# Folding the Fourier mixer's tokens n and S-n ahead of the sequence transform

## The chip, the core and the metric

The kernel runs on one NeuronCore of a Trainium2 chip. The metric is the device time of one execution in microseconds (us). The engines are named as in the profile: PE (TensorE, matmuls; PEld is its weight load), DVE (VectorE), ACT (ScalarE), POOL (GpSimd) and SP (SyncE, whose queue issues most transfers). Each engine works its own queue of instructions, and they wait for each other by semaphores.

## What is computed

One encoder layer on two requests with the same weights: 512 prompt tokens (one tile, t = 0) and 1024 sample tokens (two tiles, t = 1 and 2), 1024 channels. The part that matters here is the Fourier mixer. Its input `f` is a 512-channel slice of the input projection of the normed activations, in 4 groups of 128 channels:

```
def fourier_mix(f):
    fg = f.reshape(b, s, N_FOURIER_GROUPS, FOURIER_GROUP_DIM).astype(jnp.float32)
    y = jnp.fft.fft2(fg, axes=(1, 3), norm="ortho").real
    return y.reshape(b, s, FOURIER_WIDTH).astype(f.dtype)
...
u = rms_norm(x, norm1_g)
proj = u @ w_in
f, q, k, v, g_ret, g_a, g_b = jnp.split(proj, ...)
branch_a = fourier_mix(f) @ w_four_proj
branch_b = bidirectional_retention(q, k, v, g_ret, ret_decay_logit) @ w_ret_proj
merged = jax.nn.sigmoid(g_a) * branch_a + jax.nn.sigmoid(g_b) * branch_b
```

The real part of the two-dimensional transform is cos·cos minus sin·sin: a channel transform by a table of 65 cosine and 63 sine columns, and a sequence transform by cosine and sine tables over the tokens.

## The kernel before

Every float32 product is made of float32r halves: `split(h, l, src)` rounds on ACT (L74) and takes the remainder on DVE (L75), and `mm3` issues three matmuls (L110 to L112). Weights and tables come as slabs: `slab(src)` issues a transfer on SP's queue (L93) and splits what it brings.

The program's start goes stage by stage. `Prep` fetches the input tiles of a request (`fetch`), makes the scaled halves `uh`, `ul` (`scale`, L195 and L196), the squares and their sums (`square`, L151/L153 and L157), the norm of each token as a column (`cols`: 4 matmuls with `ones`, L130, then `nr` by a power on POOL, L134) and as a row over all partitions (`rows`: 4 matmuls, L140). `f_proj(t, g)` projects a tile to one channel group (24 matmuls of 512 columns) and `f_evac` copies the bank to `ft` on ACT (L224). `channel_dft(si, pr)` multiplies, for sequence `si` and a pair of groups `pr`, each chunk of 128 tokens of `ft` by the channel table `cs` (plain float32, L249), and evacuates with the token's norm as a scale into `zh` (ACT, L255) and `zl` (DVE, L256). `sequence_dft(si, zts)` runs over the chunks of a sequence: 4 for the prompt, 8 for the sample, 258 columns per matmul, one table slab for two chunks (prompt) or one (sample); the channel 64 has a matmul group of its own with the 4-column tile `z64`. After that come the products with `wfour`, which also combine tokens n and S-n of the result.

Between these stand the constants of the retention stage: `de` (a power on POOL), a polynomial on DVE that ends in `dz`, the small tables `ex`, and three groups of powers on POOL: `qk_dec`, `g128` and, in `decay_d`, the decay matrices `D`, four of 128x256, each as four powers of 128x64:

```
for q in range(4):
    m = slice(64 * q, 64 * (q + 1))
    nc.gpsimd.tensor_tensor(D[:, m], two.broadcast_to([P, 64]), D[:, m], op=ALU.pow)
```

The instructions are written in the order of the stages, but a scheduler sets the order on each engine's queue, by what it takes each instruction to need; the pool `fp` with 13 buffers under the tag `f2` holds `xs`, `sq`, `ft`, `zh` and `zl` in turn, and a tile waits until its buffer is free.

Of the kernel before, what the change touches and what calls it, by code (L numbers as in the profile page):

```python
# [7 lines left out]
F32 = mybir.dt.float32  # L8
F32R = mybir.dt.float32r
AF = mybir.ActivationFunctionType  # L10
ALU = mybir.AluOpType
# [3 lines left out]
P = 128  # L15
KD = 8
TC = 512
# [5 lines left out]
SEQS = ((0, 4, 0, 1), (4, 8, 1, 2))  # L23
# [7 lines left out]
C_ID, C_CS, C_POS, C_SEL, C_END = 0, 128, 256, 260, 388  # L31
# [4 lines left out]
def emit(ctx, tc, x, wsl, wup, wdq, wd0, wfour, tab, cst, rcst, vec, out):  # L36
    nc = tc.nc
# [35 lines left out]
    def split(h, l, src):  # L73
        nc.scalar.copy(h, src)  # L74
        nc.vector.tensor_tensor(l, src, h.bitcast(F32), op=ALU.subtract)  # L75
# [33 lines left out]
    def mm3(o, lh, ll, rh, rl, first, last, go_on=False):  # L109
        nc.tensor.matmul(o, lh, rh, start=first, stop=False, skip_group_check=go_on)  # L110
        nc.tensor.matmul(o, ll, rh, start=False, stop=False, skip_group_check=go_on)  # L111
        nc.tensor.matmul(o, lh, rl, start=False, stop=last, skip_group_check=go_on)  # L112
# [31 lines left out]
    class SumSq:  # L144
        def __init__(self, first=None, pool=False):
            self.acc, self.first, self.pool = None, first, pool

        def add(self, src, pool=False):
            sq = (self.first if self.acc is None and self.first is not None else tmp("sq"))[:, :src.shape[1]]
            if self.pool or pool:  # L150
                nc.gpsimd.tensor_tensor(sq, src, src, op=ALU.mult)  # L151
            else:
                nc.scalar.activation(sq, src, AF.Square)  # L153
            if self.acc is None:
                self.acc = sq
            else:
                (nc.gpsimd if self.pool else nc.vector).tensor_tensor(self.acc, self.acc, sq, op=ALU.add)  # L157
# [16 lines left out]
    class Prep:  # L174
# [23 lines left out]
            u[self.t][1].append(l)  # L198

        def square(self, k):  # L200
            self.ss.add(self.xs[k], self.t == 1 and k % 2 == 1)
            self.xs[k] = None

        def cols(self):
# [14 lines left out]

    ft = {}  # L220

    def f_evac(t, g, ps):
        ft[t, g] = fp.tile([P, TC], F32, name="ft", tag="f2")
        nc.scalar.copy(ft[t, g], ps)  # L224

    def f_proj(t, g):
        ps = bank()
        for k in range(KD):
            f_mm(ps, g, t, k)
        f_evac(t, g, ps)  # L230


    pq = {}
    z64 = [[fp.tile([P, n, 4], F32R, name=f"z64{i}{n}", bufs=1) for i in range(2)] for _, n, _, _ in SEQS]

    def channel_dft(si, pr):
        c0, ncs, t0, nt = SEQS[si]
        zt = []
        for c2 in range(ncs // 2):
            ps = bank()  # L240
            zh = fp.tile([P, 512], F32R, name="zh", tag="f2")
            zl = fp.tile([P, 512], F32R, name="zl", tag="f2")
            for j in range(2):
                c = 2 * c2 + j
                b = slice(j * 256, (j + 1) * 256)
                o = ps[:, b].rearrange("p (q g j) -> p q g j", q=2, g=2)
                for gi in range(2):
                    src = ft[t0 + c // 4, 2 * pr + gi]
                    nc.tensor.matmul(o[:, :, gi], src[:, (c % 4) * P:(c % 4 + 1) * P],  # L249
                                     cs[:, C_CS:C_CS + P], start=True, stop=True)  # L250
            for j in range(2):
                c = 2 * c2 + j
                b = slice(j * 256, (j + 1) * 256)
# [7 lines left out]
            zt.append((zh, zl))  # L261
        return zt


    def sequence_dft(si, zts):
        c0, ncs, t0, nt = SEQS[si]
# [1 line left out]
        acc = {pr: [[bank(258) for _ in range(spans)] for _ in range(2)] for pr in zts}  # L268
        acc64 = [bank(258) for _ in range(spans)] if 1 in zts else []
        per = 4 // (2 * spans)  # L270
        for c in range(ncs):
            if c % per == 0:
                th, tl = slab(tab[si * 2 + c // per], 1032)
            b = (c % 2) * 256
            for pr, zt in zts.items():
                zh, zl = zt[c // 2]
                for q in range(2):
                    for s in range(spans):
                        col = ((c % per) * 2 * spans + q * spans + s) * 258
                        m = slice(b + q * P, b + (q + 1) * P)  # L280
                        args = (th[:, col:col + 258], tl[:, col:col + 258], c == 0, c == ncs - 1)
# [58 lines left out]
    for k in range(KD):  # L340
        preps[1].fetch()
    nc.sync.dma_start(cs, cst)
    for k in range(KD):
# [5 lines left out]
    preps[0].cols()  # L349
    for g in range(4):  # L350
        f_evac(0, g, fps[g])
    for k in range(KD):
        preps[1].scale()
        preps[1].square(k)


    def small(name, cols=16):
# [32 lines left out]
    f_proj(2, 1)  # L390
    preps[2].cols()
    l2 = const.tile([P, 16], F32, name="nv", tag="nv", bufs=1)
    nc.vector.tensor_scalar(l2, z, LOG2E, None, op0=ALU.mult)

# [45 lines left out]
        decay_d(hp)  # L440
    todo = [(t, g) for g in (2, 3) for t in (1, 2)]
    for i, _ in enumerate(sequence_dft(1, {0: z10})):
        if i % 2 == 0 and todo:
            f_proj(*todo.pop(0))
    state["turn"] = -1
    for q in preps:
        q.rows()
    z11 = channel_dft(1, 1)
    fill = gb_main(range(1), fp, "f2", 13)
    next(fill)  # L450
# [878 lines left out]
```

## Time and profile before

| | us |
|---|---|
| median of 3 runs (lowest, highest) | 2277.09 (2275.61, 2282.09) |
| the profiled execution | 2278.14 |
| its span in the trace | 2276.0 |
| PE busy | 2227.3 |
| DVE busy | 1475.6 |
| ACT busy | 848.3 |
| POOL busy | 345.5 |

The granted TensorE clock is 0.991 in the mean. In the profile, times in a timeline are counted from the start of the span; a row of it gives the start, the time from the first instruction's start to the last one's end, the engine, the line, the operation with its output and inputs, and in brackets how long the engine stood before it and for whom. A plain float32 matmul of 128 columns shows as two rows. The times of matmuls overlap, so the cost of one in a stream is read from start to start.

### The profile page before, as it was taken

To read this page: it belongs to the slowest core of one execution; us is meant where nothing else is said; L and a number is where in the kernel's file an instruction comes from. 1 tells how busy PE (TensorE), PEld (TensorE's weight loads), DVE (VectorE), ACT (ScalarE), POOL (GpSimd) and SP (SyncE) were. 2 spreads that over 40 slices of the span, in tenths; PEclk is the share of its full clock that TensorE was granted. 3 is DMA by queue.
4 is the path that set the end of the run, shared out by engine and by line. 5 is a ranking of instruction groups with operands and counts; after the bars stand their busy time and mean duration, and the time that the engine had idled before them with its cause. 6 is when DMAs were issued, how large, how long until landed. Compare 5 with 4: busy or idle time off the path is not lost. (4 is left out here: it accounts for less than half of the span.)

```text
span 2276.0 us, 29369 instructions
## 1 busy us (share of the span) xinstructions
PE 2227.3 (98%) x11294; PEld 1868.5 (82%) x11294; DVE 1475.6 (65%) x2555; ACT 848.3 (37%) x1373; POOL 345.5 (15%) x184
## 2 busy tenths in 40 slices
PE   8899999999999999999999999999998999999997
PEld 6788888888888888878887788888876778999986
DVE  7454434656556462245678886767699888999744
ACT  6251222223121221233334544434453445666423
POOL 2799601111212120010110000000000000000001
PEclk9999999999999999999999999999999999999999
DMA  5252220111102012276656462323264455323562
GB/s 190 66 164 90 92 86 2 47 38 38 47 14 71 1 56 79 74 241 226 226 181 226 147 215 90 114 93 116 84 235 144 153 203 195 106 99 112 170 205 70
DMA packets 103531, 273.30 MB, mean 120 GB/s; under 512 B 11488, under 2 KB 14816, under 8 KB 97760
## 3 DMA queue, kind: packets, MB, share of 16 engines
q1 hardware_dynamic: 99936, 265.15, 34.8%
q10 hardware_dynamic: 3456, 6.29, 0.7%
q8 instruction: 88, 1.44, 0.3%
q14 instruction: 51, 0.42, 0.1%
HBM read 208.22 MB, written 63.18 MB: 119 GB/s over the span
## 5 line engine op out<-in xcount | busy, mean ns | idle before, releaser
L111 PE MATMUL bank<-op,wl 128*128 128x512 f32 (+1 forms) x1320 | 463.8, 351 | 5.8 <-DVE wl L75 5.8
L110 PE MATMUL bank<-op,wh 128*128 128x512 f32 (+1 forms) x1320 | 462.4, 352 | 3.6 <-DVE y L1099 1.7
L112 PE MATMUL bank<-op,wh 128*128 128x512 f32 (+1 forms) x1320 | 462.1, 351 | 0.5 <-DVE op L75 0.5
L75 DVE TENSOR_TENSOR wl<-wr,wh 128x1024 fp32r<-128x1024 f32 (+5 forms) x210 | 250.9, 1196 | 161.6 <-ACT wh L74 159.4
L74 ACT CAST wh<-wr 128x1024 fp32r<-128x1024 f32 (+5 forms) x210 | 204.8, 976 | 321.3 <-PE bank L112 211.1
L110 PEld LDWEIGHTS bank<-op,wh 128*128 128x128 f32 x1320 | 250.3, 190 | 42.7 <-DVE y L1099 2.6
L111 PEld LDWEIGHTS bank<-op,wl 128*128 128x128 f32 x1320 | 250.5, 190 | 41.5 <-DVE wl L75 6.6
L112 PEld LDWEIGHTS bank<-op,wh 128*128 128x128 f32 x1320 | 250.7, 190 | 36.5 <-DVE op L75 1.2
L110 PE MATMUL bank<-uh,wh 128*128 128x512 f32 x672 | 271.8, 404 | 5.1 <-ACT wh L74 5.1
L111 PE MATMUL bank<-uh,wl 128*128 128x512 f32 x672 | 266.1, 396 | 0.7 <-DVE wl L75 0.6
L112 PE MATMUL bank<-ul,wh 128*128 128x512 f32 x672 | 266.3, 396 | 0.0
L134 POOL TENSOR_TENSOR nr<-nv,mhalf 128x4 f32<-128x4 f32 (+1 forms) x10 | 12.8, 1284 | 1105.4 <-DVE nv L133 1074.8
L74 ACT CAST wh<-wt 128x1024 fp32r<-128x1024 f32 (+2 forms) x120 | 117.3, 977 | 141.9 <-PE bank L112 130.1
L425 POOL TENSOR_TENSOR D<-two,D 128x64 f32<-128x64 f32 x16 | 170.1, 10659 | 0.0
L110 PE MATMUL bank<-wh,uh 128*128 128x512 f32 x384 | 166.8, 434 | 0.0
L110 PEld LDWEIGHTS bank<-uh,wh 128*128 128x128 f32 x672 | 126.9, 189 | 31.8 <-ACT wh L74 5.1
L111 PE MATMUL bank<-wh,ul 128*128 128x512 f32 x384 | 151.6, 395 | 0.0
L112 PE MATMUL bank<-wl,uh 128*128 128x512 f32 x384 | 151.2, 394 | 0.0
L112 PEld LDWEIGHTS bank<-ul,wh 128*128 128x128 f32 x672 | 126.7, 188 | 29.2
L111 PEld LDWEIGHTS bank<-uh,wl 128*128 128x128 f32 x672 | 126.9, 189 | 28.5 <-DVE wl L75 1.6
L75 DVE TENSOR_TENSOR wl<-wt,wh 128x1024 fp32r<-128x1024 f32 (+2 forms) x120 | 135.7, 1131 | 6.5 <-ACT wh L74 6.3
L310 DVE TENSOR_TENSOR sg<-bank,rrow 128x512 f32<-128x512 f32 x48 | 33.2, 691 | 164.4 <-PE bank L112 164.4
(233 smaller groups left out, 4113.3 us busy)
## 6 DMA issues: line engine op xcount, KB each, us to landing
wr<-wsl SPq DMA_DIRECT2D x92, 512.0 KB, 3.9
wr<-wup SPq DMA_DIRECT2D x44, 1024.0 KB, 4.9
xs<-x SPq DMA_DIRECT2D x48, 256.0 KB, 4.4
wr<-tab SPq DMA_DIRECT2D x18, 516.0 KB, 3.7
wr<-wdq SPq DMA_DIRECT2D x12, 768.0 KB, 4.2
wr<-wd SPq DMA_DIRECT2D x16, 512.0 KB, 4.3
sb<-sg ACTq DMA_DIRECT2D x24, 256.0 KB, 2.0
ma<-sg SPq DMA_DIRECT2D x24, 256.0 KB, 2.0
```

The costliest lines, as they stand in the source:

```text
L74: nc.scalar.copy(h, src)
L75: nc.vector.tensor_tensor(l, src, h.bitcast(F32), op=ALU.subtract)
L110: nc.tensor.matmul(o, lh, rh, start=first, stop=False, skip_group_check=go_on)
L111: nc.tensor.matmul(o, ll, rh, start=False, stop=False, skip_group_check=go_on)
L112: nc.tensor.matmul(o, lh, rl, start=False, stop=last, skip_group_check=go_on)
L134: nc.gpsimd.tensor_tensor(r, v, mhalf[:, 0:n], op=ALU.pow)
L310: nc.vector.tensor_tensor(sg, ps, rrow[t], op=ALU.mult)
L425: nc.gpsimd.tensor_tensor(D[:, m], two.broadcast_to([P, 64]), D[:, m], op=ALU.pow)
```

## The change

The input of the transform is real, so tokens n and S-n can be added (for the cosine part) or subtracted (for the sine part) before the sequence transform, which then needs half the tokens. The change does this inside the channel transform: `f_evac` multiplies the bank by the norm's row on DVE, writes the upper half of the sequence in reverse order into `ft`, puts the token S/2 into a column of its own, `fx`, and clears the column that has no partner by a memset on POOL. `channel_dft` issues two matmuls for each group, one with `cs` and one with `cr` (the cosine columns, and the sine columns negated) on the reversed half, into the same bank. The token S/2 comes in through a rank-one product with `mid`, a row of alternating 1 and -1. `sequence_dft` runs over half the chunks and half the table slabs, and asks for the next slab behind the matmuls of a chunk instead of ahead of the next one. Since `ft` now holds normed values, the norm's rows are needed early: `rows()` of each request is called before its first `f_evac`; the scaling in the channel transform's evacuation goes away. The squares of the tiles 1 and 2 are written in place.

```
-        def add(self, src, pool=False):
-            sq = (self.first if self.acc is None and self.first is not None else tmp("sq"))[:, :src.shape[1]]
+        def add(self, src, pool=False, inplace=False):
+            if inplace:
+                sq = src
+            else:
+                sq = (self.first if self.acc is None and self.first is not None else tmp("sq"))[:, :src.shape[1]]
...
     def f_evac(t, g, ps):
-        ft[t, g] = fp.tile([P, TC], F32, name="ft", tag="f2")
-        nc.scalar.copy(ft[t, g], ps)
-
-    def f_proj(t, g):
+
+        f = ft[t, g] = fp.tile([P, TC], F32, name="ft", tag="f2")
+        r = rrow[t]
+        lo = (TC // 2, TC, 0)[t]
+        if lo:
+            nc.vector.tensor_tensor(f[:, :lo], ps[:, :lo], r[:, :lo], op=ALU.mult)
+        if lo < TC:
+            nc.vector.tensor_tensor(f[:, lo + 1:], ps[:, TC - 1:lo:-1], r[:, TC - 1:lo:-1], op=ALU.mult)
+            nc.vector.scalar_tensor_tensor(fx[min(t, 1)][g], ps[:, lo:lo + 1], (TC * (1 + min(t, 1)) * 128.0) ** -0.5,
+                                           r[:, lo:lo + 1], op0=ALU.mult, op1=ALU.mult)
+            nc.gpsimd.memset(f[:, lo:lo + 1], 0.0)
...
     def channel_dft(si, pr):
         c0, ncs, t0, nt = SEQS[si]
+        half = ncs // 2
         zt = []
-        for c2 in range(ncs // 2):
+
+        for c2 in range(half // 2):
...
-                    src = ft[t0 + c // 4, 2 * pr + gi]
-                    nc.tensor.matmul(o[:, :, gi], src[:, (c % 4) * P:(c % 4 + 1) * P],
-                                     cs[:, C_CS:C_CS + P], start=True, stop=True)
-            for j in range(2):
-                c = 2 * c2 + j
-                b = slice(j * 256, (j + 1) * 256)
-                r = rcol[t0 + c // 4][:, c % 4:c % 4 + 1]
-                nc.scalar.activation(zh[:, b], ps[:, b], AF.Identity, scale=r)
-                nc.vector.scalar_tensor_tensor(zl[:, b], ps[:, b], r, zh.bitcast(F32)[:, b],
-                                               op0=ALU.mult, op1=ALU.subtract)
+                    g = 2 * pr + gi
+                    up = ft[t0 + nt - 1, g][:, (nt == 1) * 256:]
+                    m = slice(c * P, (c + 1) * P)
+                    nc.tensor.matmul(o[:, :, gi], ft[t0, g][:, m], cs[:, C_CS:C_CS + P], start=True, stop=False)
+                    nc.tensor.matmul(o[:, :, gi], up[:, m], cr, start=False, stop=True)
+            split(zh, zl, ps)
...
+        for gi in range(2):
+            nc.tensor.matmul(o[:, :, gi], fx[si][2 * pr + gi], cs[:, C_CS:C_CS + P], start=True, stop=True)
...
     def sequence_dft(si, zts):
...
-        for c in range(ncs):
-            if c % per == 0:
-                th, tl = slab(tab[si * 2 + c // per], 1032)
+        half = ncs // 2
+        mid = fp.tile([P, TC], F32R, name="mid", tag="f2")[0:1, :258]
+        nc.scalar.copy(mid.rearrange("p (a b) -> p a b", b=2), pm[0:1].unsqueeze(1).broadcast_to([1, 129, 2]))
+        table = slab(tab[si * 2], 1032)
+        for c in range(half):
+            th, tl = table
...
+            for pr, zt in zts.items() if c == 0 else ():
+                zh, zl = zt[-1]
+                for s in range(spans):
+                    for i, z in enumerate((zh, zl)):
+                        nc.tensor.matmul(acc[pr][0][s], z[:, 0:P], mid, start=False, stop=False)
+                        if pr == 1:
+                            nc.tensor.matmul(acc64[s][0:4], z64[si][i][0:1, half], mid, start=False, stop=False)
+            if (c + 1) % per == 0 and c + 1 < half:
+                table = slab(tab[si * 2 + (c + 1) // per], 1032)
...
-    f_proj(1, 0)
     z00 = channel_dft(0, 0)
-    f_proj(1, 1)
     z01 = channel_dft(0, 1)
-    preps[1].cols()
+    preps[1].rows()
+    for g in range(2):
+        f_evac(1, g, f1[g])
     for k in range(KD):
         preps[2].scale()
-    for i, _ in enumerate(sequence_dft(0, {0: z00, 1: z01})):
-        preps[2].square(2 * i)
-        preps[2].square(2 * i + 1)
-    f_proj(2, 0)
+        preps[2].square(k)
+    sdft = sequence_dft(0, {0: z00, 1: z01})
+    f2 = [f_bank(2, 0)]
+    next(sdft)
+    preps[2].cols()
+    f2.append(f_bank(2, 1))
+    preps[2].rows()
+    for g in range(2):
+        f_evac(2, g, f2[g])
+    for _ in sdft:
+        pass
```

What the scheduler makes of it at three places. First POOL's queue around the powers, before (`nr` is the third column norm, `qbd0` and `qbd1` are tiles of the retention stage, numbers are those of the buffers):

```order
L134 TENSOR_TENSOR nr_864<-nv_863,mhalf_72 128x4
L407 TENSOR_TENSOR qk_dec_874<-two_74,ex_869 128x32
L406 TENSOR_TENSOR g128_878<-two_74,gx_875 128x8
L425 TENSOR_TENSOR D_935<-two_74,D_935 128x64 x4
L425 TENSOR_TENSOR D_944<-two_74,D_944 128x64 x4
L425 TENSOR_TENSOR D_953<-two_74,D_953 128x64 x4
L425 TENSOR_TENSOR D_962<-two_74,D_962 128x64 x4
L510 MEMSET qbd0_2940 128x256
L510 MEMSET qbd1_2942 128x256
```

The same stretch of POOL's queue after:

```order
L416 TENSOR_TENSOR de_579<-two_74,nv_578 128x16
L238 MEMSET ft_806 128x1
L134 TENSOR_TENSOR nr_771<-nv_770,mhalf_72 128x4
L463 TENSOR_TENSOR qk_dec_875<-two_74,ex_870 128x32
L462 TENSOR_TENSOR g128_879<-two_74,gx_876 128x8
L481 TENSOR_TENSOR D_922<-two_74,D_922 128x64 x4
L481 TENSOR_TENSOR D_931<-two_74,D_931 128x64 x4
L481 TENSOR_TENSOR D_940<-two_74,D_940 128x64 x4
L481 TENSOR_TENSOR D_949<-two_74,D_949 128x64 x4
L238 MEMSET ft_810 128x1
L238 MEMSET ft_1062 128x1
L238 MEMSET ft_1148 128x1
```

Three of the four memsets of tile 2 (`ft_810`, `ft_1062`, `ft_1148`) stand behind the 16 powers, `ft_806` ahead of them; `de` and the squares, which in the kernel before are spread, all stand ahead of the third `nr`. Of the two memsets at the end of the rows of before, the first waits for no semaphore.

Second PE's queue where the channel transform of the sample's first pair begins, with what each row waits for; before, behind the third column norm:

```order
L112 MATMUL bank_831<-ul_662,wh_257 128x512
L130 MATMUL bank_858<-ones_68,sq_691 128x1 [waits DVE_49,Pool_49]
L130 MATMUL bank_858<-ones_68,sq_691 128x1 x3
L249 MATMUL bank_883<-cs_66,ft_543 128x2x64 [waits DVE_49]
L249 MATMUL bank_883<-cs_66,ft_596 128x2x64
```

and after, where that norm, `rows()` and the rest of the prompt's sequence transform stand ahead:

```order
L344 MATMUL bank_848<-m64_845,cs_66 128x258 [waits Activation_49]
L274 MATMUL bank_884<-cs_66,ft_655 128x2x64 [waits DVE_49]
L275 MATMUL bank_884<-cr_196,ft_806 128x2x64
L274 MATMUL bank_884<-cs_66,ft_657 128x2x64
L275 MATMUL bank_884<-cr_196,ft_810 128x2x64 [waits DVE_49,Pool_49]
```

The fourth matmul now waits for POOL; the instruction on POOL by which its count is reached is the memset of `ft_810`.

Third DVE's queue at the first splits of the prompt's sequence transform, before (`wl` is a table's remainder, `de` and `dz` belong to the decay constants):

```order
L196 SCALAR_TENSOR_TENSOR ul<-xs,vc,uh 128x512 [waits DMAHW3_49]
L75 TENSOR_TENSOR wl<-wr,wh 128x1032 [waits DMAHW4_49]
L380 TENSOR_SCALAR dz<-de 128x16
L381 RECIPROCAL dz_497<-dz 128x16 [waits DVE_49]
L256 SCALAR_TENSOR_TENSOR zl<-bank,nr,zh 128x256 [waits Activation_49]
```

and after:

```order
L289 CAST z_201<-zx 1x2 [waits DVE_49]
L438 TENSOR_SCALAR dz<-de 128x16 [waits Pool_49]
L439 RECIPROCAL dz_581<-dz 128x16 [waits DVE_49]
L440 TENSOR_TENSOR dz<-de,dz_581 128x16 [waits DVE_49]
L441 TENSOR_TENSOR dz_581<-dz 128x16 [waits DVE_49]
L75 TENSOR_TENSOR zl<-bank,zh 128x512 [waits Activation_49]
```

`dz` stands ahead of the second pair's `zl` and waits for POOL's `de`, which has moved behind the squares of tile 2.

More of the change, by code (lines that the diff above doesn't have):

```diff
@@ L200, in square @@
         def square(self, k):
-            self.ss.add(self.xs[k], self.t == 1 and k % 2 == 1)
+            self.ss.add(self.xs[k], self.t == 1 and k % 2 == 1, self.t > 0)
             self.xs[k] = None
@@ L220, in emit, with f_bank @@
     ft = {}
+    fx = [[fp.tile([P, 1], F32, name=f"fx{si}{g}", bufs=1) for g in range(4)] for si in range(2)]
     def f_evac(t, g, ps):
-        ft[t, g] = fp.tile([P, TC], F32, name="ft", tag="f2")
-        nc.scalar.copy(ft[t, g], ps)
-    def f_proj(t, g):
+        f = ft[t, g] = fp.tile([P, TC], F32, name="ft", tag="f2")
[8 more added lines that the diff above has]
+            nc.gpsimd.memset(f[:, lo:lo + 1], 0.0)
+    def f_bank(t, g):
         ps = bank()
@@ L229, in f_proj @@
             f_mm(ps, g, t, k)
-        f_evac(t, g, ps)
+        return ps
+    def f_proj(t, g):
+        f_evac(t, g, f_bank(t, g))
+    cr = fp.tile([P, P], F32, name="cr", bufs=1)
+    pm = fp.tile([P, 2], F32, name="pm", bufs=1)
+    nc.gpsimd.memset(pm[:, 0:1], 1.0)
+    nc.gpsimd.memset(pm[:, 1:2], -1.0)
     pq = {}
-    z64 = [[fp.tile([P, n, 4], F32R, name=f"z64{i}{n}", bufs=1) for i in range(2)] for _, n, _, _ in SEQS]
+    z64 = [[fp.tile([P, n // 2 + 1, 4], F32R, name=f"z64{i}{n}", bufs=1) for i in range(2)] for _, n, _, _ in SEQS]
     def channel_dft(si, pr):
         c0, ncs, t0, nt = SEQS[si]
+        half = ncs // 2
         zt = []
-        for c2 in range(ncs // 2):
+        for c2 in range(half // 2):
             ps = bank()
@@ L244, in channel_dft @@
                 c = 2 * c2 + j
[L245 to L246 removed]
+                o = ps[:, j * 256:(j + 1) * 256].rearrange("p (q g j) -> p q g j", q=2, g=2)
                 for gi in range(2):
[L248 to L257 removed]
+                    g = 2 * pr + gi
[4 more added lines that the diff above has]
+            split(zh, zl, ps)
             for z, zz in ((zh, z64[si][0]), (zl, z64[si][1])):
@@ L261, in channel_dft @@
             zt.append((zh, zl))
+        ps = bank(256)
+        zx = fp.tile([P, TC], F32R, name="zx", tag="f2")
+        zh, zl = zx[0:1, 0:256], zx[0:1, 256:512]
+        o = ps[0:1].rearrange("p (q g j) -> p q g j", q=2, g=2)
+        for gi in range(2):
+            nc.tensor.matmul(o[:, :, gi], fx[si][2 * pr + gi], cs[:, C_CS:C_CS + P], start=True, stop=True)
+        split(zh, zl, ps[0:1])
+        for z, zz in ((zh, z64[si][0]), (zl, z64[si][1])):
+            nc.vector.tensor_copy(zz[0:1, half, 2 * pr:2 * pr + 2],
+                                  z.bitcast(F32).rearrange("p (q x) -> p q x", q=2)[:, 1, 0:128:64])
+        zt.append((zh, zl))
         return zt
@@ L280, in sequence_dft @@
                         m = slice(b + q * P, b + (q + 1) * P)
-                        args = (th[:, col:col + 258], tl[:, col:col + 258], c == 0, c == ncs - 1)
+                        args = (th[:, col:col + 258], tl[:, col:col + 258], c == 0, c == half - 1)
                         mm3(acc[pr][q][s], zh[:, m], zl[:, m], *args)
@@ L342, in emit @@
     nc.sync.dma_start(cs, cst)
+    nc.gpsimd.tensor_copy(cr[:, :65], cs[:, C_CS:C_CS + 65])
+    nc.gpsimd.tensor_scalar(cr[:, 65:], cs[:, C_CS + 65:C_CS + P], -1.0, None, op0=ALU.mult)
     for k in range(KD):
@@ L349, in emit @@
     preps[0].cols()
+    for k in range(4):
+        preps[1].scale()
+        preps[1].square(k)
+    for k in range(4, KD):
+        preps[1].scale()
+    f1 = [f_bank(1, 0)]
+    preps[0].rows()
     for g in range(4):
         f_evac(0, g, fps[g])
-    for k in range(KD):
-        preps[1].scale()
+    for k in range(4, KD):
         preps[1].square(k)
+    f1.append(f_bank(1, 1))
+    preps[1].cols()
     def small(name, cols=16):
@@ L389, in emit @@
     nc.vector.tensor_tensor(z, z, pl, op=ALU.subtract)
-    f_proj(2, 1)
-    preps[2].cols()
     l2 = const.tile([P, 16], F32, name="nv", tag="nv", bufs=1)
@@ L442, in emit @@
     for i, _ in enumerate(sequence_dft(1, {0: z10})):
-        if i % 2 == 0 and todo:
-            f_proj(*todo.pop(0))
+        f_proj(*todo.pop(0))
     state["turn"] = -1
-    for q in preps:
-        q.rows()
     z11 = channel_dft(1, 1)
```

## The prediction, made before the changed kernel was run

> **What bounds the kernel now.** I read the page's first lines, then the busy time by stage, then PE's waits in the stage that the change touches, then the queues of GpSimd (POOL) and TensorE (PE) there row by row. The page first: time and instruction counts of each engine, and from its table of groups the row of the decay powers.
>
> ```profile
> span 2276.0 us, 29369 instructions
> PE 2227.3 (98%) x11294; PEld 1868.5 (82%) x11294; DVE 1475.6 (65%) x2555; ACT 848.3 (37%) x1373; POOL 345.5 (15%) x184
> L425 POOL TENSOR_TENSOR D<-two,D 128x64 f32<-128x64 f32 x16 | 170.1, 10659 | 0.0
> ```
>
> PE is the bound: 48.7 us of the span are without a matmul. POOL has 184 instructions, and 16 of them, the powers that make the decay matrices `D`, are half of its busy time at 10.66 us each. Busy time in three stretches (up to the last column norm; to the end of the Fourier part; the rest), PE first, then the others in the order of the page:
>
> ```profile
> 0.00:82.20 82.20, 64.44 (x302) 52.70 (x303) 55.47 (x92) 40.26 (x72) 28.55 (x29) 0.92 0.43 144
> 83.00:163.70 80.70, 80.06 (x502) 68.89 (x501) 42.16 (x96) 36.65 (x58) 79.22 (x10) 1.00 0.44 134
> 163.70:2276.00 2112.30, 2081.97 (x10485) 1746.17 (x10484) 1377.95 (x2368) 770.92 (x1244) 237.70 (x146) 0.99 0.35 119
> ```
>
> Slack on PE is in the first stretch alone of the two that the change edits (64.44 of 82.20 us). In the second PE is full, and POOL, busy 79.22 of 80.70 us, runs beside it. What PE waited for in the first 164 us, in total, how often, and the longest:
>
> ```profile
> PE bank L112 <- DVE wl L75: 11.4, 3, 8.5
> PE bank L110 <- ACT wh L74: 6.2, 2, 5.1
> ```
>
> The 5.1 us are the start of the program; the rest are table splits. Now the row on which my forecast hangs: POOL's timeline from 83 us (start, length, operation), and one row of what reads `D`.
>
> ```profile
> 83.53 1.02 POOL L134 TENSOR_TENSOR nr<-nv,mhalf 128x4 f32<-128x4 f32 x1 [14.30 <-DVE nv L133]
> 85.50 5.44 POOL L407 TENSOR_TENSOR qk_dec<-two,ex 128x32 f32<-128x32 f32 x1 [0.95 <-DVE ex L399]
> 90.91 1.74 POOL L406 TENSOR_TENSOR g<-two,gx 128x8 f32<-128x8 f32 x1
> 92.50 170.08 POOL L425 TENSOR_TENSOR D<-two,D 128x64 f32<-128x64 f32 x16
> 262.53 0.56 POOL L510 MEMSET qbd<- 128x256 f32 x2
> L569 DVE SCALAR_TENSOR_TENSOR sT<-bank,D x48: 391/424/426, 347.3 to 818.7; 128x256 f32<-128x256 f32 x48
> ```
>
> The powers hold POOL from 92.50 to 262.6 us without a gap. In the kernel before this is free: `D` is first read at 347.3 us, and all that is queued behind the powers are two memsets for the retention stage.
>
> **Part 1, POOL's new rows: the wait.** `f_evac` now clears one column of `ft` by a GpSimd memset wherever it folds a tile, and the channel transform's second matmul of each pair reads that tile. By the order of the changed program the memset of `ft_810` (tile 2, group 1) stands behind all 16 powers, and the PE row `L275 MATMUL bank_884<-cr_196,ft_810` waits for POOL. PE has then issued three matmuls of the second sequence's channel transform, and everything after stands behind the fourth. That PE doesn't go round a waiting matmul shows in its rows below: between 57.05 and 65.79 us it stood for one table half, though 48 projection matmuls that need no table were queued a few rows behind.
>
> ```profile
> 49.63 0.51 PE L112 MATMUL bank<-wl,zh 128*128 128x258 f32 x1 [2.48 <-DVE wl L75]
> 53.07 0.33 PE L110 MATMUL bank<-wh,zh 128*128 128x258 f32 x1
> 57.05 0.28 PE L111 MATMUL bank<-wh,zl 128*128 128x258 f32 x1
> 65.79 1.01 PE L112 MATMUL bank<-wl,zh 128*128 128x258 f32 x3 [8.46 <-DVE wl L75]
> 70.34 0.70 PE L303 MATMUL bank<-m,cs 4*128 4x258 f32 x2
> 82.23 0.95 PE L130 MATMUL bank<-ones,sq 128*128 128x1 f32 x8
> 83.04 3.82 PE L249 MATMUL bank<-cs,ft 128*128 128x128 f32 x32
> 88.14 0.40 PE L110 MATMUL bank<-uh,wh 128*128 128x512 f32 x1
> 93.73 0.28 PE L110 MATMUL bank<-wh,zh 128*128 128x258 f32 x1
> 103.19 0.28 PE L110 MATMUL bank<-wh,zh 128*128 128x258 f32 x1
> 104.51 0.28 PE L112 MATMUL bank<-wl,zh 128*128 128x258 f32 x1
> 121.98 2.84 PE L140 MATMUL bank<-cs,nr 128*128 128x128 f32 x24
> 124.65 3.74 PE L249 MATMUL bank<-cs,ft 128*128 128x128 f32 x32
> 163.75 0.39 PE L110 MATMUL bank<-pqh,wh 128*128 128x258 f32 x1
> ```
>
> For POOL the row is the memset pair at 262.53: its first memset waits for nothing in the order, and yet began the moment the powers ended. [...]
>
> Behind the waiting matmul on PE stand all later ones; the next evacuation of ACT (`zh`) and split of DVE (`zl`) wait for it in turn, and SP's table loads stop when both raw buffers are full. So the wait covers no work.
>
> Prices from these rows: a 258-column matmul (1.32 us for 11 steps from 103.19) 0.120 us; a 512-column one (5.59 us for 24 from 88.14) 0.233; a two-pass f32 one of 128 columns (2.67 us for 12 `L140`, two rows each, up to 124.65) 0.222. When do the powers start? In the profile 10.27 us after the third column norm (82.23 to 92.50: norm, `nr`, `ex`, `qk_dec`, `g`), and this tail of the chain is kept. So I need that norm's new place:
>
> - Work ahead of it: out go one projection of 24 matmuls (5.59) and 60 - 21 = 39 of 258 columns (4.68) and two `L303` (0.63); in come 8 `L140` (1.78) and 4 for the token S/2 (0.89). Net -8.2 us: 74.0, if the stalls of this stretch stay as large.
> - Without the stalls of the wait list (11.4, and 6.2 - 5.1 = 1.1) it is 61.5, and without the slow clock behind them, 2.0 us after the long one (21 matmuls from 65.79 to 70.34 in 4.55 us, not 2.5) and 1.5 after the first (16 from 49.63 to 53.07), 58. That is the lower end.
> - Between them, by POOL's own work before that norm:
>
> ```profile
> L151 POOL TENSOR_TENSOR sq<-xs 128x512 f32<-128x512 f32 x12 | 14.2, 1192 | 0.2
> L157 POOL TENSOR_TENSOR sq<-sq 128x512 f32<-128x512 f32 x7 | 8.9, 1269 | 0.1
> L365 POOL TENSOR_TENSOR de<-two,nv 128x16 f32<-128x16 f32 x1 | 3.2, 3207 | 0.4 <-DMA rs<-rcst 0.4
> L134 POOL TENSOR_TENSOR nr<-nv,mhalf 128x4 f32<-128x4 f32 x2 | 2.4, 1198 | 39.5 <-DMA wr<-tab 30.6 <-DVE nv L133 8.9
> 54.47 5.77 DVE L386 SCALAR_TENSOR_TENSOR dp<-dp,dz 128x16 f32<-128x16 f32 x6
> 63.38 2.35 DVE L75 TENSOR_TENSOR wl<-wr,wh 128x1032 fp32r<-128x1032 f32 x1
> ```
>
> These 28.7 us can start at about 22 (the in-place squares need the scaled halves first) and are now in the way early: the DVE row that makes `dz` stands ahead of the `zl` split, so PE's first sequence transform waits for `de` behind all squares. That gives 51 at least; POOL waits for DVE twice on the way (behind nine additions of the sums, and behind the `f_evac` rows that DVE took from ACT). I estimate 9 us for both, so `de` at 60, then 15 + 6 sequence matmuls at 0.120 to 0.217 and the split before them: norm at 66, inside 58 to 74. That DVE runs slower beside POOL (six 16-element steps 5.77 us, a split 2.35) is why I don't take the low end.
>
> So the powers start at 66 + 10.3 = 76.3, end at 246.4, and PE resumes at **246.5** (238.5 to 254.5). It would have been there at about 76: a stall of some 170 us.
>
> **Part 2, after the wait.** The kernel before needed 163.75 - 83.04 = 80.7 us from the same place to the first `wfour` product. Out: 12 `L140` moved ahead (2.67), half of 240 sequence matmuls (120 x 0.120 = 14.4), three channel matmuls already issued (0.67). In: 12 rank-one matmuls with `mid` (1.44), 4 for S/2 (0.89). That is 65.3 us. The first rows run at the slow clock, as after the 8.46 us stall (+2.0 by that row), and `zh`, `zl` have to be made before the sequence matmuls (+1, an estimate: one evacuation and one split, 0.59 and 0.69 us by the two rows of Part 3, a part of it under the second bank's matmuls). [...]
>
> **Part 3, edits off the path.** Nine table transfers and their splits fall away, ACT gives its 12 copies of `ft` to DVE, and the scaled evacuations become plain ones.
>
> ```profile
> L224 ACT COPY ft<-bank x12: 562/586/596, 28.3 to 120.7; 128x512 f32<-128x512 f32 x12
> L310 DVE TENSOR_TENSOR sg<-bank,rrow 128x512 f32<-128x512 f32 x48 | 33.2, 691 | 164.4 <-PE bank L112 164.4
> ```
>
> ACT loses 12 x 0.586 = 7.0 us, DVE gains about 12 x 0.69 = 8.3; both are half idle in the second stretch, so I book nothing there; in the first the DVE load is in the norm's place above, and bare of that cover it would cost those 8.3. SP has both next tables fetched by the resume (two raw buffers), and half as many to fetch afterwards at the same rate per chunk. From the first `wfour` product on the rows of all engines are the same, so 2276.0 - 163.75 = 2112.25 us stay.
>
> Sum: 246.5 + 65.3 + 3.0 + 2112.25 = 2427.1 us of span, 151.1 more than the profile. Its own time is 2278.14, 2.1 us over its span and 1.05 over the median 2277.09; 2277.09 + 151 = **2428 us**. Ends: start of the powers 8 us either way, and 3 us either way for what follows the resume: 2417 to 2439.
>
> **Rivals.**
> - *Late norm:* DVE, slowed beside POOL as in the two rows above, gets the squares and sums out so late that the norm comes after 74 us. The doubled split (2.35 us, about twice the usual) speaks for it, the removed table waits against. At a norm at 84 the end is 2428 + 18 = 2446.
> - *Fast, the other side:* the memset is done before the powers, or PE gets past it. Then the stall is nil: 150 sequence matmuls out (18.0), 18 with `mid` (2.2) and 8 for S/2 (1.8) in, 14 us gained; of the 12.5 us of table waits and 3.5 of slow clock perhaps half go, 8 more: 2277 - 22 = 2255. One power costs 10.66 us, so this side is decided by where the memset stands: with two powers ahead of it the change gains nothing, from the third on it loses. Against it: sixteen are ahead, and the rows at 57.05 and 262.53 show neither queue passing a row.
> - *No change:* needs those two powers and no more; nothing in the order speaks for it.
>
> **How the numbers follow.** Forecast 0.83, late norm 0.10, fast 0.06, no change 0.01. The range for 8 in 10 takes the forecast's ends and a part of the late case: 2415 to 2442. About 0.3% (7 us) is what a measurement can tell from no change: faster 0.06, same 0.01, slower 0.93.
>
> **What would show it.** Right: in the changed profile PE has one idle of 150 to 180 us before a channel matmul, put down to POOL's memset; POOL's powers start at 68 to 84 us; the memset row follows them; PE's granted clock is low in four or so of the 40 slices, and DMA nearly nothing moves there; the stretch from resume to the first `wfour` product is 64 to 72 us; the split of tables counts 9. Wrong: PE idle before that matmul under 20 us (the fast rival), powers beginning after 88 us (late norm), or a second long wait later, which no row here leads me to expect.

## The result and the profile after

The changed kernel takes 2432.32 us (median of three runs, 2426.96 to 2432.45) against 2277.09: the ratio is 1.0663, 95% interval 1.0647 to 1.0679. Slower, as forecast (2428, range 2415 to 2442). The profiled execution is that of 2432.32 us, with a span of 2430.4. Times here and below are medians of the executions at the usual clock (0.958 to 0.994 in the mean of an execution); one of the ten of the kernel with two powers ahead took 3132.98 us at a granted clock of 0.652 and is left out.

First the page of the changed kernel: span, busy time of the engines, the 40 slices for PE, its granted clock and the DMA share, and two rows of the table of groups.

```profile
span 2430.4 us, 29071 instructions
PE 2220.5 (91%) x11178; PEld 1856.7 (76%) x11178; DVE 1467.2 (60%) x2552; ACT 828.6 (34%) x1341; POOL 347.4 (14%) x196
PE   8200999999999999999999999999999999999997
PEclk9655999999999999999999999999999999999999
DMA  5000322201111111115766646222237346433462
L481 POOL TENSOR_TENSOR D<-two,D 128x64 f32<-128x64 f32 x16 | 167.8, 10516 | 0.0
L275 PE MATMUL bank<-cr,ft 128*128 128x128 f32 x48 | 11.1, 322 | 167.1 <-POOL ft L238 167.1
```

PE does 6.8 us less work than before (2220.5 against 2227.3), but 209.9 us of the span are without a matmul, where it was 48.7. Most of them lie in slices 2 to 4, which read 2, 0, 0 for PE; the clock reads 6, 5, 5 there, and the DMA row reads 0 in all three. The last row has the reason in its right half: 167.1 us of idle time before a channel matmul with `cr`, all of it put down to POOL's `ft`, L238, the memset.

What PE waited for up to the first product with `wfour` (total, times, longest):

```profile
PE bank L275 <- POOL ft L238: 167.1, 1, 167.1
PE bank L110 <- ACT wh L74: 5.0, 1, 5.0
PE bank L140 <- POOL nr L134: 3.1, 1, 3.1
PE bank L130 <- DVE rs L160: 1.5, 1, 1.5
PE bank L274 <- DVE fx L236: 0.5, 1, 0.5
```

The 11.4 us that PE stood for the table halves `wl` before are gone; the one wait of 167.1 us is new. POOL's timeline around it:

```profile
60.66 2.91 POOL L416 TENSOR_TENSOR de<-two,nv 128x16 f32<-128x16 f32 x1
63.52 0.10 POOL L238 MEMSET ft<- 128x1 f32 x1
69.29 1.01 POOL L134 TENSOR_TENSOR nr<-nv,mhalf 128x4 f32<-128x4 f32 x1 [5.67 <-DVE nv L133]
71.25 5.44 POOL L463 TENSOR_TENSOR qk_dec<-two,ex 128x32 f32<-128x32 f32 x1 [0.96 <-DVE ex L455]
76.66 1.63 POOL L462 TENSOR_TENSOR g<-two,gx 128x8 f32<-128x8 f32 x1
78.26 167.76 POOL L481 TENSOR_TENSOR D<-two,D 128x64 f32<-128x64 f32 x16
245.96 0.12 POOL L238 MEMSET ft<- 128x1 f32 x2
```

And PE's, in two pieces, around the second row norm and from the third column norm to the first product behind the stop:

```profile
54.94 2.08 PE L140 MATMUL bank<-cs,nr 128*128 128x128 f32 x8 [3.07 <-POOL nr L134]
56.67 0.77 PE L110 MATMUL bank<-uh,wh 128*128 128x512 f32 x1
57.24 0.63 PE L111 MATMUL bank<-uh,wl 128*128 128x512 f32 x1
57.67 0.63 PE L112 MATMUL bank<-ul,wh 128*128 128x512 f32 x1
...
60.65 0.42 PE L110 MATMUL bank<-uh,wh 128*128 128x512 f32 x1
60.91 0.39 PE L111 MATMUL bank<-uh,wl 128*128 128x512 f32 x1
...
67.30 1.05 PE L130 MATMUL bank<-ones,xs 128*128 128x1 f32 x8
...
246.11 0.80 PE L275 MATMUL bank<-cr,ft 128*128 128x128 f32 x2 [167.10 <-POOL ft L238]
246.70 0.63 PE L274 MATMUL bank<-cs,ft 128*128 128x128 f32 x2
247.13 0.64 PE L275 MATMUL bank<-cr,ft 128*128 128x128 f32 x2
...
251.93 0.60 PE L286 MATMUL bank<-cs,fx 128*1 128x128 f32 x4
252.46 0.39 PE L110 MATMUL bank<-wh,zh 128*128 128x258 f32 x1
```

The powers start at 78.26, the two memsets of 0.12 us follow their last at 245.96, and PE goes on 0.15 us after they start. It then runs at half speed for some 5.8 us (granted clock 0.51 from 246.1 to 251.9): a channel matmul each 0.43 us, not the 0.222 by which the prediction counted. The upper piece shows the same behind the short wait of 3.07 us: 512-column matmuls 0.43 us apart up to 60.65 (granted clock 0.50 from 54.9 to 60.6), and 0.23 after (0.99 from 60.65 to 64).

Busy time by stage (PE first, then the others in the order of the page; the sixth and seventh figures are the granted clock and the DMA share):

```profile
67.30:78.60 11.30, 10.65 (x62) 8.88 (x62) 8.30 (x41) 3.32 (x8) 8.35 (x4) 1.00 0.00 0
78.60:246.10 167.50, 0.41 (x4) 0.22 (x2) 3.08 (x8) 0.00 (x0) 167.49 (x18) 0.51 0.01 3
246.10:314.00 67.90, 67.89 (x371) 57.04 (x372) 28.53 (x57) 21.89 (x35) 0.65 (x3) 0.96 0.34 105
314.00:2430.40 2116.40, 2084.08 (x10485) 1744.23 (x10483) 1376.00 (x2362) 771.21 (x1242) 137.27 (x134) 0.99 0.35 118
```

In the second row everything but POOL stands still: PE 0.41, DVE 3.08 and ACT 0.00 of 167.5 us, and 3 GB/s on the DMA queues. One instruction of 0.1 us had a whole core behind it. From 246.10 on, behind these 5.8 us at the slow clock, the kernel does what it would have done from 78.6.

### The profile page after: what moved, and what is told of

Read it like the earlier page. It is cut to its first block, busy times and chain, and to the rows that moved or that the text cites. A ratio compares the mean times of both kernels' runs of the same rounds, so it can differ in the third digit from the quotient of the medians.

```text
span 2430.4 us, 29071 instructions
## 1 busy us (share of the span) xinstructions
PE 2220.5 (91%) x11178; PEld 1856.7 (76%) x11178; DVE 1467.2 (60%) x2552; ACT 828.6 (34%) x1341; POOL 347.4 (14%) x196
## 5 line engine op out<-in xcount | busy, mean ns | idle before, releaser
L110 PE MATMUL bank<-op,wh 128*128 128x512 f32 (+1 forms) x1320 | 462.3, 352 | 3.2 <-DVE y L1152 2.2
L75 DVE TENSOR_TENSOR wl<-wr,wh 128x1024 fp32r<-128x1024 f32 (+5 forms) x201 | 240.4, 1197 | 149.9 <-ACT wh L74 147.9
L74 ACT CAST wh<-wr 128x1024 fp32r<-128x1024 f32 (+5 forms) x201 | 195.3, 973 | 330.3 <-PE bank L112 223.2
L110 PEld LDWEIGHTS bank<-op,wh 128*128 128x128 f32 x1320 | 250.4, 190 | 42.6 <-DVE y L1152 3.5
L110 PE MATMUL bank<-uh,wh 128*128 128x512 f32 x672 | 273.9, 408 | 5.0 <-ACT wh L74 5.0
L481 POOL TENSOR_TENSOR D<-two,D 128x64 f32<-128x64 f32 x16 | 167.8, 10516 | 0.0
L110 PE MATMUL bank<-wh,uh 128*128 128x512 f32 x384 | 166.7, 434 | 0.0
L275 PE MATMUL bank<-cr,ft 128*128 128x128 f32 x48 | 11.1, 322 | 167.1 <-POOL ft L238 167.1
L110 PEld LDWEIGHTS bank<-uh,wh 128*128 128x128 f32 x672 | 127.9, 190 | 33.1 <-ACT wh L74 5.0
L111 PEld LDWEIGHTS bank<-uh,wl 128*128 128x128 f32 x672 | 127.7, 190 | 28.7 <-DVE wl L75 0.8
```

The source lines that it names most:

```text
L275: nc.tensor.matmul(o[:, :, gi], up[:, m], cr, start=False, stop=True)
```

## The experiments

All kernels below are the changed kernel with the edit shown. (The last but one is the kernel before.) Ratios are to the kernel before, run on the same chip beside them (there 2280.3 to 2281.0 us). For each, the time of the first product with `wfour` is the start of the group `L110 bank<-pqh,wh` in its trace; it was 163.7 us before and 314.0 after, and it separates the stage that the change edits from the long rest.

**The memset on another engine.**

```
-            nc.gpsimd.memset(f[:, lo:lo + 1], 0.0)
+            nc.vector.memset(f[:, lo:lo + 1], 0.0)
```

> The changed kernel with one edit: VectorE instead of GpSimd clears the column of ft. Theory (PE's 167 us are the wait for a memset that stands behind sixteen powers in GpSimd's queue): the idle and the slow clock behind it go, 2432 - 167 - 2 = about 2263 us, and by the sum of the prediction 2255; range 2248 to 2268, so faster than the kernel before by 0.4 to 1.3%; the powers keep their place in GpSimd's queue and run beside PE. Rival 1 (the wait has another cause, such as the norm's row, the bank or the buffer of ft, and the memset is merely what the view names): 2420 to 2440. Rival 2 (the powers are in somebody else's way too, and another wait for GpSimd takes the place of this one): 2290 to 2420, with a PE idle of over 20 us put down to GpSimd.

Measured 2263.27 us, ratio 0.9925 [0.9906, 0.9944]. What PE waited for in the first 142 us:

```profile
PE bank L110 <- ACT wh L74: 5.1, 1, 5.1
PE bank L140 <- POOL nr L134: 2.1, 1, 2.1
PE bank L110 <- DVE zl L75: 1.5, 1, 1.5
PE bank L110 <- DVE zx L75: 0.4, 1, 0.4
```

The wait is gone, with nothing in its place, and the first product comes at 142.2. The powers stand where they stood (75.98 to 245.87 us) and now run beside PE. So the memset was the cause, not only the name in the view, and the rest of the change is a gain: the kernel before needs 21.5 us more to that point. The same stretch in both kernels, before and then this one, shows where these come from:

```profile
0.00:163.70 163.70, 145.29 (x810) 122.36 (x810) 97.62 (x188) 77.42 (x130) 107.77 (x39) 0.96 0.43 139
```

```profile
0.00:142.20 142.20, 132.94 (x694) 109.44 (x695) 91.65 (x198) 57.43 (x99) 107.63 (x43) 0.98 0.40 130
```

PE is busy 12.35 us less, with 116 rows fewer, and idle 9.26 us instead of 18.41.

**The memset on POOL, the powers behind it.** Written later in the code, the powers keep their place in the order of POOL's rows: it is set by what each row needs. So they get something to need, a base that is made from the second pair's `zh`:

```
-            nc.gpsimd.tensor_tensor(D[:, m], two.broadcast_to([P, 64]), D[:, m], op=ALU.pow)
...
     z11 = channel_dft(1, 1)
+    late = const.tile([P, 1], F32, name="late")
+    nc.vector.tensor_scalar(late, z11[1][0].bitcast(F32)[:, 0:1], 0.0, 2.0, op0=ALU.mult, op1=ALU.add)
+    powers(range(0, 16), late)
```

(`powers` holds the line taken out, with the base as an argument.)

> The memsets stay on GpSimd, but all sixteen powers read their base, 2.0, from a tile that VectorE makes from the second pair's zh of the sample's channel transform; so all memsets of ft stand ahead of the powers in GpSimd's queue. Theory: as with the memset on VectorE, 2250 to 2268 us; the powers then start at some 115 to 125 us, last 168 to 170 and end near 290, ahead of the first reader of D at about 325. Rival 1 (it is the memset itself on GpSimd that is slow to reach, whatever stands ahead of it): 2420 to 2440. Rival 2 (the late powers are late for their readers, D or the memsets of qbd): 2270 to 2300.

Measured 2256.69 us, ratio 0.9904 [0.9883, 0.9924]. POOL's timeline:

```profile
78.37 0.12 POOL L238 MEMSET ft<- 128x1 f32 x2
81.43 0.10 POOL L238 MEMSET ft<- 128x1 f32 x1 [2.94 <-PE bank L274]
118.67 168.24 POOL L498 TENSOR_TENSOR D<-late,D 128x64 f32<-128x64 f32 x16 [37.14 <-DVE late L506]
286.84 0.57 POOL L569 MEMSET qbd<- 128x256 f32 x2
```

The same memset on the same engine costs nothing once it stands ahead; the first product comes at 144.1. The powers end at 286.9 us, ahead of their first reader (327.6 us in this trace).

**The dose.** The same edit, with 2 and with 8 of the 16 powers keeping the early base, and so ahead of the memset:

```
+    powers(range(2), two)
...
+    powers(range(2, 16), late)
```

> As the kernel with all powers behind, but two of the sixteen powers keep the base that is ready early and so stand ahead of the memset. Theory (the price is what is left of the powers when PE gets there): PE idles 2 x 10.5 - 0.7 = 20.3 us before the fourth matmul of the sample's channel transform, and with 2 us of slow clock the time is 20 to 23 us over that of the kernel with none ahead: about 2277 to 2283 us, the same as the kernel before within 0.3% (the break-even of the prediction). Rival (the price is fixed, paid as soon as the order is wrong): near 2430; or (PE has other work to cover the first 20 us): 2255 to 2262, as with none ahead.

> The same with eight of the sixteen powers ahead of the memset. Theory: PE idles 8 x 10.5 - 0.7 = 83 us, and the time is 83 to 87 us over that of the kernel with none ahead: about 2338 to 2350 us. Rival (a fixed price): near 2430. Rival (the later half of the powers adds a second wait, since it runs beside full PE work): over 2355.

With two, 2281.39 us, ratio 1.0004 [0.9995, 1.0014]; with eight, 2343.20, ratio 1.0281 [1.0257, 1.0304]. PE's longest wait in the one and in the other:

```profile
PE bank L275 <- POOL ft L238: 19.4, 1, 19.4
```

```profile
PE bank L275 <- POOL ft L238: 82.3, 1, 82.3
```

| powers ahead | PE idle for the memset, us | first product with `wfour` at | later than with none, beyond the idle | time, us |
|---|---|---|---|---|
| 0 | 0 | 144.1 | | 2256.69 |
| 2 | 19.4 | 167.5 | 4.0 | 2281.39 |
| 8 | 82.3 | 228.8 | 2.4 | 2343.20 |
| 16 (the changed kernel) | 167.1 | 314.0 | 2.8 | 2432.32 |

Each power ahead costs PE 10.5 to 10.6 us (62.9 for six, 84.8 for eight), and a stop costs 2.4 to 4.0 us more. Of the 4.0, 0.9 arose ahead of the stop (the first channel matmul of the sample came at 79.05, with none ahead at 78.20). From the fourth channel matmul to the first product the kernels with 2, 8 and 16 ahead took 68.1, 67.6 and 67.9 us, against 65.1 with none: 2.5 to 3.0 us for the slow clock behind the stop (in all three the channel matmuls behind it start 0.43 us apart, up to 104.67, 166.01 and 251.40 us). Beyond that there is no fixed price. Two powers cost 24.7 us of time, a little over the expected 20 to 23, and use up what the change gains.

**One memset freed, two left.** `ft` of tile 2, group 1, gets a buffer of its own, so that its memset is ready early and stands ahead of the powers; those of groups 2 and 3 stay behind them.

```
-        f = ft[t, g] = fp.tile([P, TC], F32, name="ft", tag="f2")
+        own = dict(tag="f2own", bufs=1) if (t, g) == (2, 1) else dict(tag="f2")
+        f = ft[t, g] = fp.tile([P, TC], F32, name="ft", **own)
```

(and 12 buffers for the tag `f2`, not 13)

> The changed kernel with one edit: ft of tile 2, group 1, has a buffer of its own, and the pool f2 has 12 buffers, not 13; so its memset is ready early, and the scheduler puts it ahead of the powers, while the memsets of groups 2 and 3 stay behind them on GpSimd. Theory (in-order queue, the price is what is left of the powers when PE arrives): the wait does not go, it moves: PE runs on through the sample's first pair and stops at the first matmul with cr of the second pair, which in the kernel with all powers behind stood at 111.9 us; the powers end at about 246, so PE idles about 134 us and the time is 2257 + 134 + 3 = about 2394 us, 2385 to 2405. Rival 1 (only the first pair's memset matters, the later ones are hidden behind projections): 2255 to 2268. Rival 2 (it waits at the old place): 2420 to 2440. Rival 3 (the 12 buffers of the pool now cost a wait of their own): more than 2405.

Measured 2401.65 us, ratio 1.0525 [1.0511, 1.0539]. PE's longest wait, and the row behind it in PE's timeline:

```profile
PE bank L276 <- POOL ft L239: 135.6, 1, 135.6
```

```profile
246.73 0.80 PE L276 MATMUL bank<-cr,ft 128*128 128x128 f32 x2 [135.61 <-POOL ft L239]
```

The wait did not go, it moved: PE ran through the first pair, and stopped at the second pair's first `cr` from 111.1 to 246.7. The end was the same as in the changed kernel, the end of the powers; what PE did in between (some 32 us of work) is what was saved. It also says what put the memset behind the powers in the first place: it waited for a buffer of `f2`, and the scheduler put what was ready ahead of it.

**What the powers cost beside PE.** The kernel with the memset on VectorE, without the powers (`D` then holds the exponents).

```
-            nc.gpsimd.tensor_tensor(D[:, m], two.broadcast_to([P, 64]), D[:, m], op=ALU.pow)
```

> The changed kernel with the column cleared on VectorE, and without the sixteen powers (D keeps the exponents, so the attention's result is another one; all other work stays). It prices the powers where they run beside PE. Theory (off the path they cost nothing but a little DVE time): 2255 to 2263 us, within 3 us of the kernel with the powers; the first product with wfour at 140 to 142.5 us (142.2 with them). Rival (powers on GpSimd slow VectorE's and so PE's work beside them, or the long tail): 2235 to 2250.

Measured 2264.55 us, a little above the expected range, ratio 0.9926 [0.9912, 0.9939], against 0.9925 with the powers (2263.27 us); the first product at 142.5 against 142.2. Off the path, 170 us of GpSimd cost nothing that these runs can tell.

**A better version.** In the kernel with the powers behind, the wait list has 3.1 us for the second `nr`, which POOL makes behind squares of tile 2. These squares go to ScalarE:

```
-            if self.pool or pool:
+            if pool:
                 nc.gpsimd.tensor_tensor(sq, src, src, op=ALU.mult)
```

> A try for a better version: all powers behind the memsets (as in the kernel before with none ahead), and in addition the eight squares of tile 2 go from GpSimd to ScalarE, so that GpSimd's queue reaches the second and third column norms and de earlier. In the kernel with the powers behind, PE waits 3.1 us for the second nr and 1.4 and 0.5 us near it, each with a slow clock behind; theory: some 3 to 6 us of that go and the first product with wfour comes at 138 to 141 us, not 144.1; the time is 2250 to 2254 us, a ratio of 0.987 to 0.990. Rival (ScalarE's eight squares of about 0.6 us delay its splits of tables and zh instead): the first product at 144 to 148 us, 2256 to 2262 us.

Measured 2251.19 us, ratio 0.9868 [0.9854, 0.9881], the fastest of all. What PE waited for in the first 136 us:

```profile
PE bank L110 <- ACT wh L74: 5.1, 1, 5.1
PE bank L110 <- DVE zl L75: 0.6, 1, 0.6
PE bank L274 <- DVE fx L236: 0.5, 1, 0.5
PE bank L140 <- POOL nr L134: 0.2, 1, 0.2
```

The wait for `nr` is 0.2 us, and the first product comes at 136.5, 7.6 us earlier, where 3 to 6 were expected. The stretch up to it, with the squares on POOL and then on ScalarE (the sixth figure is the granted clock):

```profile
0.00:144.10 144.10, 133.87 (x694) 110.16 (x695) 90.88 (x191) 57.58 (x99) 67.35 (x47) 0.96 0.39 128
```

```profile
0.00:136.50 136.50, 129.93 (x694) 107.33 (x695) 86.04 (x191) 62.08 (x107) 56.47 (x39) 1.00 0.41 135
```

PE's idle time falls from 10.23 to 6.57 us, and the busy time of the same 694 rows by 3.94, with the clock up from 0.96 to 1.00. So half of the gain is the slow clock that followed the short waits; the estimate had too little of it. Of the three waits that it names, the slow clock followed those of 3.1 and 1.4 us, with 512-column matmuls 0.43 us apart, and not the one of 0.5 us: in the projection behind it they are 0.23 us apart, from 85.17 us on.

The same edit in the kernel with the memset on VectorE and the powers early:

> Two edits that were made apart so far: the column is cleared on VectorE (the powers keep their early place), and the squares of tile 2 go to ScalarE. It tells whether the late powers have a part in the best time so far (2251 us), or the squares alone. Theory (the squares took the wait for the second nr, 2.1 us here, and the slow clock behind it; the powers' place costs nothing before the first product with wfour): the first product at 135 to 139 us, against 142.2 with the squares on GpSimd, and the time 2252 to 2259 us. Rival (the powers beside the sample's transform slow VectorE's splits): the first product after 140 us.

Measured 2253.50 us, ratio 0.9884 [0.9868, 0.9901], the first product at 136.7. So the squares made the step, and the place of the powers, once no memset is behind them, has no part that can be seen.

**A difference in the long rest.** From the first product to the end the traces took 2110.3 to 2117.3 us with the same rows on PE, and the kernels with the tile `late` were on the short side. So the kernel with the memset on VectorE got this tile, one column wide, with nothing that reads it:

```
+    late = const.tile([P, 1], F32, name="late")
+    nc.vector.tensor_scalar(late, z11[1][0].bitcast(F32)[:, 0:1], 0.0, 2.0, op0=ALU.mult, op1=ALU.add)
```

> The kernel that clears the column on VectorE, plus the small tile (one column of 2.0, made from the second pair's zh) that the kernels with late powers have; here nothing reads it. It prices a difference in the long tail: from the first product with wfour to the end the four kernels that have this tile took 2110.3 to 2115.0 us, those without it 2112.3 to 2117.3, with the same rows on PE; in one stage, 384 + 768 matmuls from the first product of gh to the first of op, 275.3 us against 278.2. Theory (it is the tile, by moving what is allocated after it): that stage takes 275 to 276 us here. Rival (it is the place of the powers, or chance from run to run): 277.5 to 279 us.

Measured 2256.98 us, ratio 0.9899 [0.9884, 0.9914]. The stage named took 276.4 us, between the two forecasts, and with the other traces beside it (275.2 to 277.1 with the tile, 276.8 to 278.2 without) it was the wrong gauge. PE's busy time over the whole rest tells the kernels apart (one trace of each); here without the tile, and then with it:

```profile
142.20:2258.00 2115.80, 2083.88 (x10485) 1744.74 (x10483) 1376.71 (x2362) 771.21 (x1242) 241.12 (x146) 0.99 0.36 118
```

```profile
145.50:2257.60 2112.10, 2076.59 (x10485) 1745.07 (x10483) 1375.79 (x2362) 770.93 (x1242) 237.79 (x146) 0.99 0.36 118
```

In these two traces as a whole the difference does not show (2259.82 and 2259.38 us): with the tile the rest took 3.7 us less, but PE came to the first product 3.3 us later, behind a wait of 3.0 us for a `zl` (1.5 without it). The medians are 2263.27 and 2256.98 us, and the intervals of their ratios overlap a little.

Two more kernels tested the effect on the rest: the kernel before with the tile, and the kernel with the memset on VectorE and a tile of 16 columns.

> The kernel before, with the unread tile of one column (4 bytes of each partition, allocated among the constants) and the row on VectorE that writes it; nothing else. In eleven traces PE's busy time from the first product with wfour to the end, over the same rows, was 2076.6 to 2079.7 us in the five kernels that have this tile and 2082.0 to 2084.1 in the six that do not. Theory (the tile moves what is allocated behind it, and the matmuls run a little faster at the new places): 2076 to 2080 us here, not 2082.0, and the whole kernel 2 to 5 us faster than before, a ratio of 0.998 to 0.999. Rival (chance, or another part of those kernels): 2081 to 2085 us, ratio 1.000.

> The kernel that clears the column on VectorE, with the unread tile 16 columns wide (64 bytes of each partition) and not one. Theory A (what counts is where the later tiles begin, at a finer grain than 64 bytes): PE's busy time from the first product with wfour to the end is back at 2082 to 2085 us. Theory B (what counts is that there is a tile, or the row that writes it): 2076 to 2080 us, as with one column.

The kernel before with the tile took 2276.18 us, ratio 0.9980 [0.9971, 0.9989]; PE's busy time in the rest was 2079.8 us, not 2082.0. With 16 columns it was 2082.2 and the time 2263.27, ratio 0.9927 [0.9914, 0.9939], as without a tile. PE's busy time in the rest is 2076.6 to 2079.8 us in all six kernels with the tile of one column and 2082.0 to 2084.1 in the seven without it or with the wide one. So it goes with the tile's size, and not with there being a tile or a row more. Whether the size acts by moving what is allocated behind the tile was not shown, nor why PE's busy time over the same rows differs.

## Why the prediction was right

By its own steps, what was forecast and what the trace shows:

| step | forecast, us | measured, us |
|---|---|---|
| `de` done on POOL | 60 | 63.57 |
| third column norm on PE | 66 (58 to 74) | 67.30 |
| powers start | 76.3 | 78.26 |
| powers end | 246.4 | 246.0 |
| PE resumes | 246.5 | 246.11 |
| from there to the first product with `wfour` | 65.3 + 3.0 | 67.9 |
| from there to the end | 2112.25 | 2116.4 |
| span | 2427.1 | 2430.4 |

- **Part 1, the wait**, carried the forecast, and it was right in mechanism and size. POOL did not pass the powers, PE did not pass its matmul, and the first two experiments show that either side of the order alone removes the wait. The start of the powers was 2.0 us late (norm 1.3, the chain from norm to powers 11.0 instead of 10.3), and the powers were 2.3 us shorter than in the profile before (167.76 against 170.08). That these two misses cancel is luck. So is part of the norm's place. From 22 us to the end of `de` POOL stood for 8.9 us, as estimated (9), but worked for 32.6 and not 28.7, so `de` was done 3.6 us late; and from there to the norm it took 3.7 us instead of 6. PE did not stand for `de` either, as the sum had it: behind its wait of 3.07 us for the second `nr` it had a projection to do, half of it at the slow clock (granted clock 0.50 up to 60.6), up to 64.12, and the `zl` that `dz` held back was done at 65.09, where PE came to need it (65.14). In the kernels with the memset on VectorE and with two powers ahead it did stand 1.5 us for this `zl`. All four kernels that have powers ahead of a memset show the same order. The memset starts where the last of them ends, at 99.24 with two, 161.01 with eight, 245.96 with sixteen, and 246.58 in the kernel with a buffer of its own, and PE's waiting matmul starts 0.15 us behind it in each (99.39, 161.16, 246.11, 246.73).
- **Part 2, after the wait**, came to 67.9 us against 68.3. The 3.0 us in it for slow clock and refill came to 2.8: the kernel with no powers ahead needs 65.1 us for the same rows. Its share of slow clock was too small: the half-speed rows run from 246.11 to 251.93, 13 channel matmuls in 5.82 us (granted clock 0.51) where 13 x 0.222 = 2.9 would do, so 2.9 us and not 2.0; the refill hid better than booked, since the first product after the channel transform starts at 252.46 with no wait.
- **Part 3, the long rest**, is the term that missed: 2116.4 us, 4.2 more than was carried over from the profile before, and so more than the 3.3 us by which the span was missed; the steps ahead of it give 0.8 back. PE's busy time there went from 2081.97 to 2084.08 and its idle time from 30.3 to 32.3. The other kernels with the change and no `late` of one column have 2115.6 to 2117.3. "The same rows, so the same time" holds to some 4 us only: the tile experiments show that PE's busy time over the same rows moves by up to 7 us with one unread tile of 4 bytes per partition, and the change allocates other tiles. Whether that is the cause of these 4.2 us was not tried.
- **The fast rival** was priced at -22 us, 14 of work and 8 of stalls. With the wait taken out the first product comes 21.5 us earlier, 12.35 by PE's busy time and 9.15 by its idle time. The two kernels that take it out are 17 and 24 us faster than the kernel before, and the long rest of the second, which has the tile `late`, is 5.5 us shorter than that of the first. Its condition, that two powers ahead use the gain up, was measured at a ratio of 1.0004.
- **What the prediction left out**: the two memsets behind that of `ft_810`. They cost nothing in the changed kernel only because the first one had already waited out the powers; the kernel with its own buffer shows 135.6 us for them alone.
- **The list of signs** held: one idle of 167.1 us put down to POOL's memset, powers at 78.26 (68 to 84), memset behind them, no second long wait, nine table splits of 128x1032. The clock is low in three slices (6, 5, 5), not in four or so.

One part of the change did nothing: asking for a table behind the matmuls of a chunk, instead of ahead of the next one's, gives the same rows in the same order on all five queues. The table waits that went must have gone with another part, most simply the half of the tables that is no longer fetched; that was not tried apart.

## What to carry to other kernels

Before a cheap instruction is put on an idle engine, read that engine's queue in the order of the changed program: an engine at 15% busy held one stretch of 170 us here, and the memset that landed behind it cost PE 167.1 us. The price was what was left of the work ahead at the moment the waiter arrived, 10.5 to 10.6 us for each power, and freeing one of several such instructions only moved the wait to the next (135.6 us in the kernel with a buffer of its own). Where a scheduler sets the order by readiness, moving lines in the code may do nothing; what moves a row is what it needs, a buffer or an operand, or the engine that it runs on.

## What the runs showed of the hardware that was not expected

- The sixteen powers on GpSimd took nearly the same time with the rest of the core idle, 167.8 us, and beside full PE work, 168.2 to 170.1. Without them the first product with `wfour` came at 142.5 us, with them at 142.2.
- Half the clock came behind short stops too: in the changed kernel PE ran at half rate for 5.7 us behind a wait of 3.07 us (granted clock 0.50 from 54.9 to 60.6). Behind a wait of 1.50 us, which ended at 31.41, it ran at half rate from 33.5 to 36.6 us (granted clock 0.50), so the slow clock came 2 us after PE had resumed (0.97 in between). Taking such waits out by moving the squares gave 3.9 us of busy time beside the 3.7 us of idle time.
- A tile of 4 bytes for each partition, read by nobody, makes the kernel before 0.2% faster (0.9980 [0.9971, 0.9989]) and the kernel with the memset on VectorE 6 us faster by the medians (2256.98 against 2263.27, PE's busy time in the rest 2076.6 against 2083.9). With 64 bytes the median is 2263.27 again. A difference of a few us between two versions can be this, and not the edit.
